# A two-layer decoder trunk on one core: heads stepped before other tasks, x turned on other engines at two places, fewer low parts on POOL

## The chip, the cores and the metric

The kernel runs on one core of one Trainium2 chip. The metric is the device time of one execution in microseconds, median over runs. TensorE is called PE in the rows, VectorE DVE, ScalarE ACT, GpSimd POOL, SyncE SP.

## The reference, cut to what matters

The input x has 256 rows (tokens) of 2048 columns; mem has 256 rows as well. Each of two layers does, all in float32:

```python
h = rmsnorm(x, g);  p = h @ W_in                # columns split among four mixers
x = x + concat(A(p), B(p), C(p), D(p)) @ W_o    # A: forgetting attention (FoX), B: latent attention (MLA),
                                                # C: spatial gating unit, D: differential attention; 4 heads each
c = rmsnorm(x, g2)
x = x + cross_attention(c, rmsnorm(mem)) @ W_co # 4 heads, 256 memory rows
f = rmsnorm(x, g3)
x = x + (silu(f @ W_gate) * (f @ W_up)) @ W_down  # hidden width 5632
```

The output is the norm of the last x. The forgetting attention adds to its scores the difference of two running sums of log-forget values, one per row and one per column.

## The kernel before, in words

**Products.** Every float32 product is made of three matmuls on numbers split into a high part (rounded to the fp32r type) and a low part (what is left): high by high, high by low of the weight, low of the activation by high (lines 303, 304 and 305 in `multiply_natural`). So each weight block of 1 MB, once fetched ("raw"), is cast by ACT into `whi` (line 204), and `wlo = raw - whi` is made by DVE, or by POOL (line 210). POOL makes it for every fourth unit of the groups whose name stands in the tuple `POOLED` near the top of the file.

**Work lists.** The kernel is a long list of groups, each one a matrix product into 512 columns of output (`dq`, `m`, `dk`, ..., `v`, `u`, `wo`, `cq`, `ck`, `cv`, `wco`, `gate`, `up`, `down`). `drive` cuts the groups into units, each of two blocks of 128 rows of the weight by 512 columns: 12 matmuls. It walks through the units in order: it first converts the weights of up to three units ahead (casts and low parts), then issues the matmuls of the unit, then calls `step()`. A group may give back some of its units to be done later ("hold"): thus the first `wco` units of two chunks are interleaved.

**Tasks.** All else (attention heads, norms, turning x) is written as Python generators that are advanced by one piece for each unit. Tasks are of two kinds: `urgent`, all of which advance in each `step()`, and `background` (heads), of which the first two advance. What `step()` issues stands in the program order of its engine right there; each engine runs its instructions strictly in that order.

**x and its norms.** x lies in four chunks of 512 columns, `self.x[0..3]`. When a `wo` or `wco` group of a chunk is done, `into_x` adds its two halves from PSUM into x on DVE (line 950, two instructions of 128x512) and starts `norm_chunk` as a task: ACT forms the sums of squares, and the chunk is then turned (columns onto partitions), since it will be a stationary operand. If the argument `early` is true, DVE turns it by `turn_blocks` in 16 instructions (line 428), four of them in each step, into an SBUF buffer `xT`. Otherwise TensorE turns it in `turn` (line 419), two groups of four 128x128 matmuls into PSUM. Both are followed by `split_turned`: high parts on ACT (line 206) and low parts on DVE (line 212), one for each 128 columns, called `cT_hi`, `cT_lo` for the cross attention and `fT_hi`, `fT_lo` for the feed-forward half. A unit that needs a chunk whose task isn't finished drains that task first (`Split.need`).

**Heads.** `scores` (lines 436 to 441) issues the score matmuls of a head, over pairs of operands; it forms the part for the second 128 queries over 256 keys, and that for the first 128 queries over 128 keys, except that operands of type fp32r are always taken with 256 columns. In the differential heads a reciprocal `inv` (line 468) of the softmax's sums is taken on DVE, ACT scales by it (line 473), TensorE turns the result (line 479). In the cross attention `cpt` (line 1078) are the turned probabilities, `cpT` (line 1079) their copy on ACT, and `co` (line 1116) the products with the values.

Of the kernel before, what the change touches and what calls it, by code (L numbers as in the profile page):

```python
# [12 lines left out]
F32R = mybir.dt.float32r  # L13
# [6 lines left out]
P = 128  # L20
T = 2
S = T * P
# [3 lines left out]
NC = 4  # L26
# [10 lines left out]
LEAD = 8  # L37
O_ORDER = [4, 5, 6, 7, 12, 13, 14, 15, 0, 1, 2, 3, 8, 9, 10, 11]
RAWS = 4
POOLED = ("wco", "wo", "cq", "fk", "fv")  # L40

PI_LO = float(np.nextafter(np.float32(np.pi), np.float32(0)))
MAGIC = 1.5 * 2.0 ** 23
# [18 lines left out]
class Task:  # L62
# [5 lines left out]
    def step(self):  # L68
        if not self.done:
            try:  # L70
                next(self.gen)
            except StopIteration:
                self.done = True
# [68 lines left out]
class Kernel:  # L142
# [48 lines left out]
            yield  # L191

    def step(self):
        for t in list(self.urgent):
            t.step()
        self.urgent = [t for t in self.urgent if not t.done]
        for t in list(self.background)[:2]:
            t.step()
        self.background = deque(t for t in self.background if not t.done)


    def high(self, src, hi, scale=None):
# [24 lines left out]
    def drive(self, groups):  # L227

        units, held = [], []
        for g in groups:  # L230
            i, own = 0, []
            for src, kper in g.blocks:
                b = Block(src, kper * g.ncols)
                step = 1 if not units and not own else 1024 // g.ncols if g.ncols in (256, 512) else 2
                for k0 in range(0, kper, step):
                    n = min(step, kper - k0)
                    own.append(Unit(g, b, k0, n, i))
                    i += n
            if g.hold:
                units, held = units + own[: g.hold], own[g.hold :]  # L240
            else:
                units, held = units + own[: len(held)] + held + own[len(held) :], []
# [23 lines left out]
    def convert(self, u):  # L266
# [15 lines left out]
        u.lo = self.whl.tile([P, 1024], F32R, tag="wlo", name="wlo")  # L282
        self.split(b.raw[:, u.k0 * u.group.ncols : u.k0 * u.group.ncols + nw], u.hi[:, :nw], u.lo[:, :nw], eng=nc.gpsimd if u.group.name in POOLED and u.i % 4 == 0 else None)

# [57 lines left out]
    def norm_chunk(self, st, c, g, name, early):  # L342

        nc, xs, stats, xc = self.nc, st[0], st[1], self.x[c]
        part = xs.parts[c] = self.split_tile(name)
        for t in range(T):
            self.square_sum(xc[:, t, :], stats[:, t, c : c + 1])
        st[4] += 1
        yield
        yield  # L350
        if early:
            raw = self.slot("xT")
            yield from self.turn_blocks(xc[:], raw)
        for b in range(2):
            tv = raw[:, 2 * b : 2 * b + 2, :] if early else self.turn(xc, 2 * b, 2, "xT")
            self.split_turned(tv, part, 2 * b, self.gains[:, g, 4 * c + 2 * b : 4 * c + 2 * b + 2])
            yield
# [75 lines left out]
    def scores(self, pairs, name="s"):  # L433

        ps = self.bank(name)
        first = True
        for q, off, nk in ((1, 0, S), (0, S, P)):
            for n, (x, y) in enumerate(pairs):
                w = S if x.dtype == F32R else nk
                self.nc.tensor.matmul(ps[:, off : off + w], x[:, q * P : (q + 1) * P], y[:, :w], start=first, stop=(q == 0 and n == len(pairs) - 1))  # L440
                first = False
        return ps

# [353 lines left out]
    def mixers(self, l, norm, st, mem):  # L797

        y = Split(4)
# [140 lines left out]
        yield group("v", False, done_v)  # L940
        yield group("u", False, done_u)
        for c in range(NC):
            yield Group("wo", self.blocks("w_o", l, c), 512, y, False, self.into_x(c, st, 1 + 3 * l, "cT", c < NC - 1), O_ORDER, begin=mem if c == NC - 1 else None, hold=0 if c else 4)

    def into_x(self, c, st=None, g=None, name=None, early=False):

# [134 lines left out]
    def cross(self, l, norm, st, memT, mres):  # L1081
        s = {}
        y, cT = Split(1), norm[0]

        def out_q(ps):
            nat = self.slot("cq", shape=(P, T, 512))
            self.out_natural(ps, 0, 512, nat, self.times(norm[2][0], 128.0 ** -0.5))
            s["q"] = self.slot("cqT")
            yield
            yield from self.turn_blocks(nat[:], s["q"])  # L1090

        def done_q(ps):
            norm[3].drain()
            s["tq"] = self.soon(out_q(ps))

        def done_k(ps):
            self.mem_rms.drain()
            kT = self.slot("ckT")
            s["tk"] = self.soon(self.out_turned(ps, kT, mres[1]))
            s["p"] = [self.slot("cpT", shape=(P, 2, 512)) for _ in range(2)]  # L1100
            s["heads"] = [self.later(self.attend_memory((s["tq"], s["tk"]), s["q"], kT, h, s["p"][h // 2][:, h % 2, :])) for h in range(4)]

        def out_v(ps, hh):
            if hh == 0:
                s["v"] = self.slot("cv", shape=(P, T, 512))
                y.parts[0] = self.split_tile("yc")
            v = s["v"]
            self.out_natural(ps, 0, 256, v[:, :, 256 * hh : 256 * hh + 256], mres[0])
            yield
            for t in s["heads"][2 * hh : 2 * hh + 2]:  # L1110
                t.drain()
            o = self.bank("co")
            for i in range(2):
                h = 2 * hh + i
                for kt in range(2):
                    self.nc.tensor.matmul(o[:, i * S : (i + 1) * S], v[:, kt, h * P : (h + 1) * P], s["p"][hh][:, i, kt * S : (kt + 1) * S], start=(i == 0 and kt == 0), stop=(i == 1 and kt == 1))
            ov = o[:].rearrange("p (i s) -> p i s", i=2)
            self.split(ov, y.parts[0][0][:, 2 * hh : 2 * hh + 2, :], y.parts[0][1][:, 2 * hh : 2 * hh + 2, :])

        def done_v(hh):  # L1120
            def f(ps):
                s["tv%d" % hh] = self.soon(out_v(ps, hh))
                if hh == 1:
                    y.tasks[0] = [s["tv0"]]
                    y.late = s["tv1"]
            return f

        yield Group("cq", self.blocks("w_cq", l), 512, cT, False, done_q)
        yield Group("ck", self.blocks("w_ck", l), 512, memT, True, done_k)
        for hh in range(2):  # L1130
            yield Group("cv", self.blocks("w_cv", l, hh, 8), 256, memT, False, done_v(hh))
        for c in range(NC):
            yield Group("wco", self.blocks("w_co", l, c), 512, y, False, self.into_x(c, st, 2 + 3 * l, "fT"), hold=0 if c else 1)


    def ffn(self, l, norm, st):
# [211 lines left out]
```

## Time and profile before

| | |
|---|---|
| median of 3 runs | 2347.46 us (2346.2 to 2347.61) |
| the profiled execution | 2347.7 us |
| its span, first to last instruction | 2346.0 us |
| mean granted clock of TensorE | 0.999 |
| busy: TensorE / DVE / ACT / POOL | 99% / 64% / 48% / 11% |

The profile's times are of one profiled execution; 1.7 us of its 2347.7 lie outside the span. Times of single instructions in the rows are microseconds from the start of the span. Matmuls overlap: one of 512 columns is listed with 0.39 us, while the next starts 0.227 us after it, so that ends of matmuls are modelled and starts are what counts.

### The profile page before, as it was taken

How to read it: one execution, taken by the hardware profiler on the slowest of the kernel's cores; microseconds unless marked ns; L12 is line 12 of the kernel's file. 1: busy time of each engine (PE TensorE's matmuls, PEld its weight loads, DVE VectorE, ACT ScalarE, POOL GpSimd, SP SyncE). 2: the span in 40 equal slices, each digit the busy share in tenths (PEclk: the TensorE clock that was granted, in tenths of full speed). 3: DMA queues.
4: the chain of work that ended last, by engine and by line, in shares of the span. 5: the costliest groups of instructions: out<-in, count | busy, mean ns of one | idle time of the engine just before them, and what ended most of it. 6: DMA issues, size and time to landing. Idle time of an engine off the chain costs nothing.

```text
span 2346.0 us, 28353 instructions
## 1 busy us (share of the span) xinstructions
PE 2324.7 (99%) x10992; PEld 1950.3 (83%) x10992; DVE 1508.6 (64%) x2175; ACT 1132.2 (48%) x1611; POOL 251.3 (11%) x182
## 2 busy tenths in 40 slices
PE   9999999999999999999999999999999999999998
PEld 8888878888888888888898888798888888888886
DVE  6856687655766446767766666866666664476564
ACT  7656555644443334444455555545444443434443
POOL 1222341100000000000012314411000000000000
PEclk9999999999999999999999999999999999999999
DMA  8654555455455555555545454554555555555643
GB/s 293 223 177 154 186 189 188 164 193 200 179 208 195 189 197 181 196 200 184 203 164 193 161 176 159 201 197 162 197 180 197 202 194 196 197 180 192 221 179 126
DMA packets 69719, 444.24 MB, mean 189 GB/s; under 512 B 8000, under 2 KB 10064, under 8 KB 19920
## 3 DMA queue, kind: packets, MB, share of 16 engines
q1 hardware_dynamic: 67328, 435.52, 52.4%
q0 software_dynamic: 2112, 6.85, 0.9%
q8 instruction: 86, 1.41, 0.2%
q14 instruction: 49, 0.40, 0.0%
q10 hardware_dynamic: 144, 0.06, 0.0%
HBM read 440.30 MB, written 2.10 MB: 189 GB/s over the span
## 4 chain that ended last, share of the span: by engine, by line
PE 88%; DVE 4%; ACT 2%; DMA 2%; issue 1%; POOL 1%; SPq 0%; POOLq 0%; ACTq 0%; DVEq 0%
PE gate L305 7%; PE gate L304 7%; PE gate L303 7%; PE up L305 7%; PE up L304 7%; PE up L303 7%; PE down L303 7%; PE down L305 7%; PE down L304 7%; DVE wlo L210 1%; PE wo L305 1%; PE wo L303 1%; PE wo L304 1%; ACT whi L204 1%; DVE xT L428 1%
## 5 line engine op out<-in xcount | busy, mean ns | idle before, releaser
L210 DVE TENSOR_TENSOR wlo<-raw,whi 128x1024 fp32r<-128x1024 f32 (+3 forms) x764 | 933.5, 1235 | 572.4 <-ACT whi L204 566.2
L204 ACT CAST whi<-raw 128x1024 fp32r<-128x1024 f32 (+2 forms) x828 | 842.3, 1037 | 633.8 <-PE up L305 246.6
L303 PE MATMUL gate<-whi,fT_hi 128*128 128x512 f32 x704 | 274.7, 390 | 0.0
L305 PE MATMUL gate<-whi,fT_lo 128*128 128x512 f32 x704 | 274.0, 389 | 0.0
L304 PE MATMUL gate<-wlo,fT_hi 128*128 128x512 f32 x704 | 273.9, 389 | 0.0
L303 PE MATMUL up<-whi,fT_hi 128*128 128x512 f32 x704 | 273.9, 389 | 0.0
L304 PE MATMUL up<-wlo,fT_hi 128*128 128x512 f32 x704 | 273.9, 389 | 0.0
L305 PE MATMUL up<-whi,fT_lo 128*128 128x512 f32 x704 | 273.9, 389 | 0.0
L303 PE MATMUL down<-whi,hid_hi 128*128 128x512 f32 x704 | 273.9, 389 | 0.0
L304 PE MATMUL down<-wlo,hid_hi 128*128 128x512 f32 x704 | 273.9, 389 | 0.0
L305 PE MATMUL down<-whi,hid_lo 128*128 128x512 f32 x704 | 273.9, 389 | 0.0
L210 POOL TENSOR_TENSOR wlo<-raw,whi 128x1024 fp32r<-128x1024 f32 x64 | 165.3, 2587 | 408.4 <-ACT whi L204 408.2
L428 DVE STREAM_TRANSPOSE hidT<-silu 32x256 f32<-32x256 f32 x352 | 153.3, 436 | 5.7
L305 PEld LDWEIGHTS down<-whi,hid_lo 128*128 128x128 f32 x704 | 132.2, 188 | 27.6
L305 PEld LDWEIGHTS gate<-whi,fT_lo 128*128 128x128 f32 x704 | 132.2, 188 | 27.5
L304 PEld LDWEIGHTS up<-wlo,fT_hi 128*128 128x128 f32 x704 | 132.2, 188 | 27.5
L303 PEld LDWEIGHTS up<-whi,fT_hi 128*128 128x128 f32 x704 | 132.2, 188 | 27.5
L305 PEld LDWEIGHTS up<-whi,fT_lo 128*128 128x128 f32 x704 | 132.2, 188 | 27.3
L304 PEld LDWEIGHTS down<-wlo,hid_hi 128*128 128x128 f32 x704 | 132.2, 188 | 27.3
L303 PEld LDWEIGHTS down<-whi,hid_hi 128*128 128x128 f32 x704 | 132.2, 188 | 27.3
L304 PEld LDWEIGHTS gate<-wlo,fT_hi 128*128 128x128 f32 x704 | 132.2, 188 | 27.2
L303 PEld LDWEIGHTS gate<-whi,fT_hi 128*128 128x128 f32 x704 | 132.2, 188 | 27.2
(426 smaller groups left out, 3347.1 us busy)
## 6 DMA issues: line engine op xcount, KB each, us to landing
raw<-in_w_gate SPq DMA_DIRECT2D x88, 1024.0 KB, 4.8
raw<-in_w_up SPq DMA_DIRECT2D x88, 1024.0 KB, 4.7
raw<-in_w_down SPq DMA_DIRECT2D x88, 1024.0 KB, 4.8
raw<-in_w_o SPq DMA_DIRECT2D x32, 1024.0 KB, 4.8
raw<-in_w_dk SPq DMA_DIRECT2D x8, 1024.0 KB, 5.1
raw<-in_w_dv SPq DMA_DIRECT2D x8, 1024.0 KB, 6.5
raw<-in_w_fq SPq DMA_DIRECT2D x8, 1024.0 KB, 4.9
raw<-in_w_fk SPq DMA_DIRECT2D x8, 1024.0 KB, 4.8
```

The lines of the kernel that those rows point to most:

```text
L204: self.nc.scalar.copy(hi, src)
L210: (eng or self.nc.vector).tensor_tensor(out=lo, in0=src, in1=hi.bitcast(F32), op=ALU.subtract)
L303: mm(o, xh, wh, start=(i == 0), stop=False)
L304: mm(o, xh, wl, start=False, stop=False)
L305: mm(o, xl, wh, start=False, stop=(i == len(g.ks) - 1))
L428: self.nc.vector.transpose(o[:, :, :, a, :], src[32 * a : 32 * a + 32, :, :, b, :])
```

## The change

It has six parts:

1. `wo` and `cq` leave `POOLED`: all their low parts are made by DVE.
2. `step()` advances the two background tasks (heads) first and the urgent tasks after them.
3. In `norm_chunk`, a chunk turned on DVE waits one more step between the last transpositions and the split.
4. In `scores`, the second part has 128 columns for operands of type fp32r too.
5. After `wo`, all four chunks are turned on TensorE (before, chunks 0 to 2 on DVE).
6. After `wco`, chunks 0 and 1 are turned on DVE (before, all four on TensorE).

```diff
--- before.py
+++ after.py
@@ -37,7 +37,7 @@
 LEAD = 8
 O_ORDER = [4, 5, 6, 7, 12, 13, 14, 15, 0, 1, 2, 3, 8, 9, 10, 11]
 RAWS = 4
-POOLED = ("wco", "wo", "cq", "fk", "fv")
+POOLED = ("wco", "fk", "fv")
 
 PI_LO = float(np.nextafter(np.float32(np.pi), np.float32(0)))
 MAGIC = 1.5 * 2.0 ** 23
@@ -191,12 +191,12 @@
             yield
 
     def step(self):
+        for t in list(self.background)[:2]:
+            t.step()
+        self.background = deque(t for t in self.background if not t.done)
         for t in list(self.urgent):
             t.step()
         self.urgent = [t for t in self.urgent if not t.done]
-        for t in list(self.background)[:2]:
-            t.step()
-        self.background = deque(t for t in self.background if not t.done)
 
 
     def high(self, src, hi, scale=None):
@@ -351,6 +351,7 @@
         if early:
             raw = self.slot("xT")
             yield from self.turn_blocks(xc[:], raw)
+            yield
         for b in range(2):
             tv = raw[:, 2 * b : 2 * b + 2, :] if early else self.turn(xc, 2 * b, 2, "xT")
             self.split_turned(tv, part, 2 * b, self.gains[:, g, 4 * c + 2 * b : 4 * c + 2 * b + 2])
@@ -436,8 +437,7 @@
         first = True
         for q, off, nk in ((1, 0, S), (0, S, P)):
             for n, (x, y) in enumerate(pairs):
-                w = S if x.dtype == F32R else nk
-                self.nc.tensor.matmul(ps[:, off : off + w], x[:, q * P : (q + 1) * P], y[:, :w], start=first, stop=(q == 0 and n == len(pairs) - 1))
+                self.nc.tensor.matmul(ps[:, off : off + nk], x[:, q * P : (q + 1) * P], y[:, :nk], start=first, stop=(q == 0 and n == len(pairs) - 1))
                 first = False
         return ps
 
@@ -940,7 +940,7 @@
         yield group("v", False, done_v)
         yield group("u", False, done_u)
         for c in range(NC):
-            yield Group("wo", self.blocks("w_o", l, c), 512, y, False, self.into_x(c, st, 1 + 3 * l, "cT", c < NC - 1), O_ORDER, begin=mem if c == NC - 1 else None, hold=0 if c else 4)
+            yield Group("wo", self.blocks("w_o", l, c), 512, y, False, self.into_x(c, st, 1 + 3 * l, "cT"), O_ORDER, begin=mem if c == NC - 1 else None, hold=0 if c else 4)
 
     def into_x(self, c, st=None, g=None, name=None, early=False):
 
@@ -1130,7 +1130,7 @@
         for hh in range(2):
             yield Group("cv", self.blocks("w_cv", l, hh, 8), 256, memT, False, done_v(hh))
         for c in range(NC):
-            yield Group("wco", self.blocks("w_co", l, c), 512, y, False, self.into_x(c, st, 2 + 3 * l, "fT"), hold=0 if c else 1)
+            yield Group("wco", self.blocks("w_co", l, c), 512, y, False, self.into_x(c, st, 2 + 3 * l, "fT", c < 2), hold=0 if c else 1)
 
 
     def ffn(self, l, norm, st):
```

In the changed file the lines from 354 to 438 stand one higher than before (line 428 is now 429, 419 is 420), the later ones where they were. At three places the order of an engine's instructions shows what moved. In the names, the number behind `x` is the chunk (`x0_113` is chunk 0 of x).

**DVE, end of `wco`, first layer.** `fT_lo_4099`, `fT_lo_4125` and `fT_lo_4195` are the low parts of chunks 0, 1 and 2, the `wlo` are those of the first `gate` weights. Before:

```order
L212 SCALAR_TENSOR_TENSOR fT_lo_4099<-xT_4147,gains_91,fT_hi_4098 128x256 x2
L210 TENSOR_TENSOR wlo_4159<-raw_3957,whi_4158 128x1024
L950 TENSOR_TENSOR x2_115<-wco_4134,x2_115 128x512 x2
L212 SCALAR_TENSOR_TENSOR fT_lo_4099<-xT_4176,gains_91,fT_hi_4098 128x256 x2
L212 SCALAR_TENSOR_TENSOR fT_lo_4125<-xT_4185,gains_91,fT_hi_4124 128x256 x2
L210 TENSOR_TENSOR wlo_4201<-raw_3957,whi_4200 128x1024
L212 SCALAR_TENSOR_TENSOR fT_lo_4125<-xT_4217,gains_91,fT_hi_4124 128x256 x2
L210 TENSOR_TENSOR wlo_4229<-raw_4061,whi_4228 128x1024
L950 TENSOR_TENSOR x3_116<-wco_4204,x3_116 128x512 x2
L212 SCALAR_TENSOR_TENSOR fT_lo_4195<-xT_4246,gains_91,fT_hi_4194 128x256 x2
```

After; `fT_lo_4161` are low parts of chunk 2, `fT_lo_4078` those of chunk 0, which the first `gate` unit multiplies:

```order
L429 STREAM_TRANSPOSE xT_4126<-x0_113 32x2x4x32 x4
L429 STREAM_TRANSPOSE xT_4155<-x1_114 32x2x4x32 x4
L210 TENSOR_TENSOR wlo_4167<-raw_3918,whi_4166 128x1024
L429 STREAM_TRANSPOSE xT_4126<-x0_113 32x2x4x32 x4
L429 STREAM_TRANSPOSE xT_4155<-x1_114 32x2x4x32 x4
L210 TENSOR_TENSOR wlo_4194<-raw_4040,whi_4193 128x1024
L950 TENSOR_TENSOR x3_116<-wco_4170,x3_116 128x512 x2
L429 STREAM_TRANSPOSE xT_4126<-x0_113 32x2x4x32 x4
L429 STREAM_TRANSPOSE xT_4155<-x1_114 32x2x4x32 x4
L212 SCALAR_TENSOR_TENSOR fT_lo_4161<-xT_4219,gains_91,fT_hi_4160 128x256 x2
L210 TENSOR_TENSOR wlo_4235<-raw_4040,whi_4234 128x1024
L212 SCALAR_TENSOR_TENSOR fT_lo_4078<-xT_4126,gains_91,fT_hi_4077 128x256 x4
```

The transpositions of chunks 0 and 1 (line 429) have come onto DVE, four in a step; chunk 0's last four and its low parts stand behind the add of chunk 3, where before chunk 0's low parts stood around the add of chunk 2.

**TensorE, the second pair of heads of the cross attention, first layer**, the piece of the difference where `cpt` moves (a `-` row is of the kernel before, a `+` row of the changed one):

```order
-L305 MATMUL cv<-whi,memTs_lo 128x256
-L1078 MATMUL cpt<-ident,cp 128x128 x8
 L303 MATMUL wco<-whi,yc_hi 128x512
 L304 MATMUL wco<-wlo,yc_hi 128x512
@@ -2055,4 +2060,5 @@
 L304 MATMUL wco<-wlo,yc_hi 128x512
 L305 MATMUL wco<-whi,yc_lo 128x512
+L1078 MATMUL cpt<-ident,cp 128x128 x8
 L1116 MATMUL co<-cpT,cv 128x256 x4
 L303 MATMUL wco<-whi,yc_hi 128x512
```

`cpt` has moved down by one unit of `wco`, to right in front of the `co` that reads its copy; the same holds for the first pair, and for both in the second layer.

**DVE, the stage of `u`, first layer**: `inv` is the reciprocal for a differential head, `v` the gating unit's norm, `yd_lo` low parts of finished heads. Before:

```order
L777 SCALAR_TENSOR_TENSOR v<-v,lnr,lnw 128x512
L212 SCALAR_TENSOR_TENSOR yd_lo<-ydT,gsm,yd_hi 128x512
L468 RECIPROCAL inv<-sums 128x2
L212 SCALAR_TENSOR_TENSOR yd_lo<-ydT,gsm,yd_hi 128x512
L210 TENSOR_TENSOR wlo<-raw,whi 128x1024
```

After:

```order
L210 TENSOR_TENSOR wlo<-raw,whi 128x1024
L429 STREAM_TRANSPOSE ydT<-on 32x2x4x32 x4
L468 RECIPROCAL inv<-sums 128x2
L776 SCALAR_TENSOR_TENSOR v<-v,mv,lnw 128x512
L777 SCALAR_TENSOR_TENSOR v<-v,lnr,lnw 128x512
L210 TENSOR_TENSOR wlo<-raw,whi 128x1024
L212 SCALAR_TENSOR_TENSOR yd_lo<-ydT,gsm,yd_hi 128x512
```

The reciprocal has moved ahead of two instructions for `v` and of the first `yd_lo`.

## Rows read from the trace of the kernel before

**Rows 1.** The page, part 1: busy time, share of the span, instructions.

```profile
PE 2324.7 (99%) x10992; PEld 1950.3 (83%) x10992; DVE 1508.6 (64%) x2175; ACT 1132.2 (48%) x1611; POOL 251.3 (11%) x182
```

**Rows 2.** The page, chain that ended last, by engine.

```profile
PE 88%; DVE 4%; ACT 2%; DMA 2%; issue 1%; POOL 1%; SPq 0%; POOLq 0%; ACTq 0%; DVEq 0%
```

**Rows 3.** Waits of PE: us in total, times, longest us.

```profile
PE wo L304 <- DVE wlo L210: 3.5, 4, 1.5
PE fpt L479 <- ACT fp L473: 3.0, 2, 1.5
PE cq L304 <- POOL wlo L210: 1.2, 3, 0.6
PE fo L500 <- ACT fptt L483: 1.1, 2, 0.6
```

**Rows 4.** Timeline of PE in wo: start us, us, engine, instruction [idle before].

```profile
323.45 0.39 PE L303 MATMUL wo<-whi,ys_hi 128*128 128x512 f32 x1
...
325.30 0.50 PE L304 MATMUL wo<-wlo,ys_hi 128*128 128x512 f32 x1 [1.46 <-DVE wlo L210]
325.63 0.40 PE L305 MATMUL wo<-whi,ys_lo 128*128 128x512 f32 x1
```

**Rows 5.** Timeline of DVE and POOL in wo.

```profile
314.61 2.96 POOL L210 TENSOR_TENSOR wlo<-raw,whi 128x1024 fp32r<-128x1024 f32 x1 [3.28 <-ACT whi L204]
...
315.23 5.16 DVE L212 SCALAR_TENSOR_TENSOR cT_lo<-xT,gains,cT_hi 128x256 fp32r<-128x256 f32 x2
...
325.27 1.79 DVE L428 STREAM_TRANSPOSE xT<-x 32x256 f32<-32x256 f32 x4
```

**Rows 6.** Timeline of DVE and PE in the stage of u.

```profile
248.11 0.75 DVE L777 SCALAR_TENSOR_TENSOR v<-v,lnr,lnw 128x512 f32<-128x512 f32 x1
...
249.44 0.16 DVE L468 RECIPROCAL inv<-sums 128x2 f32<-128x2 f32 x1
...
250.55 0.33 PE L479 MATMUL fpt<-ident,fp 128*128 128x128 f32 x1 [1.51 <-ACT fp L473]
```

**Rows 7.** Lines by form, DVE and ACT: busy us, mean ns, idle before.

```profile
L210 DVE TENSOR_TENSOR wlo<-raw,whi 128x1024 fp32r<-128x1024 f32 x724 | 899.0, 1254 | 553.2 <-ACT whi L204 547.4
...
L428 DVE STREAM_TRANSPOSE xT<-x 32x256 f32<-32x256 f32 x144 | 62.7, 436 | 2.2
...
L212 DVE SCALAR_TENSOR_TENSOR fT_lo<-xT,gains,fT_hi 128x256 fp32r<-128x256 f32 x32 | 13.8, 478 | 3.1 <-ACT fT_hi L206 3.1
...
L204 ACT CAST whi<-raw 128x1024 fp32r<-128x1024 f32 x788 | 813.3, 1051 | 621.1 <-PE up L305 246.6 <-PE down L305 203.4 <-PE gate L305 116.5
...
L206 ACT ACTIVATE fT_hi<-xT,gains 128x256 fp32r<-128x256 f32 x32 | 13.2, 472 | 11.1 <-PE xT L419 11.1
```

**Rows 8.** Timeline of PE and ACT, first heads of the cross attention.

```profile
411.24 1.04 PE L1078 MATMUL cpt<-ident,cp 128*128 128x128 f32 x8
...
412.17 1.07 ACT L1079 COPY cpT<-cpt 128x512 f32<-128x512 f32 x2
```

**Rows 9.** Lines by form, PE: scores of FoX.

```profile
L440 PE MATMUL fs<-rows,own 128*128 128x256 f32 x16 | 6.1, 384 | 0.0
```

**Rows 10.** Timeline of DVE in wco.

```profile
444.01 1.22 DVE L210 TENSOR_TENSOR wlo<-raw,whi 128x1024 fp32r<-128x1024 f32 x1 [1.95 <-ACT whi L204]
...
454.12 1.28 DVE L950 TENSOR_TENSOR x<-wco,x 128x512 f32<-128x512 f32 x2
```

**Rows 11.** Timeline of PE from wco to gate.

```profile
453.37 0.60 PE L419 MATMUL xT<-ident,x 128*128 128x128 f32 x4
453.73 0.48 PE L303 MATMUL gate<-whi,fT_hi 128*128 128x512 f32 x1
```

**Rows 12.** Cores: span and mean granted clock of PE.

```profile
core 0: 2346.0 us, clock 0.999
```

**Rows 13.** Timeline of PE at the start.

```profile
1.11 3.79 PE L588 MATMUL idle<-ones 128*128 128x128 f32 x16 [1.11 <-DVE mhalf L584]
...
6.49 0.39 PE L303 MATMUL dq<-whi,hT_hi 128*128 128x512 f32 x1
```

## The prediction, made before the change was run

> **What bounds the kernel now.** First the page's busy times: TensorE is busy for 2324.7 of 2346.0 us [rows 1]. The reader is to see that hardly 1% is left to gain by better cover, and that any time in which TensorE stands is lost whole. Then the chain of waits: 88% of it is TensorE [rows 2]. Third, TensorE's waits by releaser, which name every place where it stands. Four kinds matter here, 11 waits: 3.5 us in wo for a low part on DVE, 3.0 in u for a softmax, 1.2 in cq for a low part on POOL, 1.1 in front of fo [rows 3]. The rest is a steady stream: a matmul of 512 columns starts every 0.227 us (each weight matrix is worked off in units of 12 such matmuls, 12 x 0.227 = 2.72 us).
>
> **What such a wait really costs** is read from two starts. In wo a matmul starts at 323.45 and the one two places on at 325.63: 2.18 us where 2 x 0.227 = 0.45 is normal, so 1.72 lost where the list says 1.46 [rows 4]. The ends are modelled, so I add 0.26 to each listed wait.
>
> **The change, part by part.**
>
> *POOL without wo and cq.* 32 low parts of wo and 8 of cq go to DVE at 1.25 us each [rows 7]. What they leave behind is the reason for the waits: while POOL writes a low part for 2.96 us, two instructions of DVE beside it take 5.16 us [rows 5], where the same shape takes 2 x 0.478 undisturbed [rows 7]. With that gone I count wo's waits (3.5 + 4 x 0.26 = 4.5) and cq's (1.2 + 3 x 0.26 = 2.0) as gained. The 40 x 1.25 = 50 us on DVE are hidden as long as DVE, 64% busy [rows 1], keeps ahead of TensorE in wo and cq; it is rid there of the 2 x 3 x 16 = 96 transpositions of the fourth part below. If that cover is gone, the 6.5 us stay.
>
> *Heads first in a step.* In u the softmax's reciprocal stands on DVE behind v (0.75 us) and a low part of yd, at 249.44, and TensorE's fpt waits for it until 250.55 [rows 6]. The order after the change puts the reciprocal ahead of both, about 1.5 us earlier, which is the whole wait: 3.0 + 2 x 0.26 = 3.5 gained in two layers. In front of fo another matmul pair of 0.65 us now stands between the transposition and its reader, nearly the whole of each wait; 1.1 + 2 x 0.26 less 0.1 each = 1.4 gained. On the other side, the order puts co's first four matmuls directly behind the eight transpositions of cpt, in four places. Before, a unit lay between: cpt at 411.24, its copies on ACT from 412.17 [rows 8], a unit of matmuls, and then co. A copy is half of 1.07 = 0.54 us, ends about 0.3 us after the transpositions in the best case and later by one copy at worst; I take 0.5 for each: **+2.0** (bounds 0.5 and 4).
>
> *Scores with 128 columns.* 8 of the 16 matmuls of 128x256 [rows 9] become 128x128. None can give back more than half of its 384 ns, 8 x 0.19 = 1.5 in all; but matmuls overlap, and matmuls of 128x128 start 0.13 us apart [rows 8], about a third of 384 ns as it is, so most of that isn't there to be had. If the weight load behind a short one shows, it costs at most that 0.13, 1.0 in all. Between -1.5 and +1.0 I take 0.
>
> *Chunks for the cross attention on TensorE, two of the four for the feed-forward half on DVE.* 3 x 2 groups of four transpositions come to TensorE in each layer and 2 x 2 leave it: 4 more groups over both layers. A group takes 453.37 to 453.73, 0.36, and a slower start of the next matmul, 0.1 [rows 11]: 4 x 0.45 = **+1.8**.
>
> *The new wait, at gate.* Here the change costs most. The first gate unit needs chunk 0's high and low parts. Until now TensorE turned it. Now DVE does, in 16 instructions, four in a step, and the order shows the last four on DVE behind the add of chunk 3, the last of the stage. I lay DVE's queue out from where it last waits, the low part that starts at 444.01 [rows 10]; each four transpositions take 1.79 [rows 5] and a low part 1.25 [rows 7], an add of two halves 1.28 [rows 10]:
> - low part until 445.3, 4 of chunk 0 until 447.1, low part 448.3, add of chunk 2 449.6, 4 + 4 transpositions 453.2, low part 454.4, 4 + 4 458.0, low part 459.2, add of chunk 3 460.5;
> - 4 + 4 464.1 (chunk 0 is complete at 462.3), two low parts of chunk 2 at 0.48 465.0, low part 466.2, first low part of chunk 0 466.7.
>
> TensorE's side: before, the wco stage ended with four transpositions at 453.37, and gate began at 453.73 [rows 11]. Four groups of transpositions (chunks 0 and 1) fall away from that stretch, 4 x 0.45 = 1.8, so gate could begin at 451.9. Its first two matmuls need high parts alone; the third, due 2 x 0.227 later at 452.4, needs the low part. 466.7 - 452.4 = **14.3 us** lost.
>
> The third gate unit needs chunk 1. After the wait TensorE has 10 matmuls, a group of transpositions, a unit and the first group of chunk 3: 466.7 + 2.27 + 0.45 + 2.72 + 0.45 = 472.6, and the matmul with the low part is due at 473.1. But ACT has chunk 1's high parts behind those of chunk 3, which wait for that group, and a cast; DVE has a weight's low part ahead. From 472.6: two high parts 0.94 [rows 7], the cast 1.05 [rows 7], the weight's low part 1.25, chunk 1's 0.48, and some 0.5 for the steps between the engines: 476.8, so **3.7 us**. Together 18.0 a layer, **+36.0**.
>
> At least so much is lost: chunk 3 can't be added before TensorE has finished it, 454.12 [rows 10] less 1.8 = 452.3; then the add 1.28, eight transpositions 3.58, two low parts of chunk 2 0.96, a low part 1.25 and chunk 0's 0.48 end at 459.9, even with an empty queue ahead: 7.5 us.
>
> The price of a transposition decides the queue: 28 lie between 445.3 and 466.7. The rows have 436 ns for one [rows 7], and four in 1.79 us [rows 5]. The Trainium skill ("VectorE: DVE Perf Modes", section "The three transpose paths") gives VectorE 311 ns and TensorE 390 for a transposition; by an estimate from its 311, 28 of them would take 8.7 us and not 12.5, the wait 10.5 and the total 7.6 less than mine, 2373.9. The trace's row is for this very instruction, so I go by it.
>
> *The clock.* TensorE has no long stop in the run before; its mean granted clock was 0.999 [rows 12]. What it does after standing is seen only at the start: 16 transposition-size matmuls in 3.79 us, 0.24 each from 1.11 on [rows 13], where eight later take 1.04, 0.13 each [rows 8]: half speed, the lower of its two levels; at 6.49 a matmul takes 0.39 us [rows 13], as everywhere later. So some 5.4 us ran at half speed: 2.7 lost. I take a stop of 14 us to be like that start, once a layer: **+5.4** (bounds 0, and 10.8 if the wait for chunk 1 does the same). The Trainium skill ("TensorE: Matmul & The Clock Gate", section "Why this matters for your kernels") warns of idle gaps between bursts of matmuls, since the clock falls in them; no row of this trace has such a gap in mid-run, and without that the sum is the first rival's.
>
> **The sum**, against the profiled execution's 2347.7 us (0.24 above the median of 2347.46; the difference is left out): gains 4.5 + 2.0 + 3.5 + 1.4 = 11.4; 2347.7 - 11.4 + 2.0 + 1.8 + 36.0 + 5.4 = **2381.5 us**, 1.4% slower.
>
> **The rivals.**
> - *The clock holds through the gap*: 2381.5 - 5.4 = 2376.1. For it: only the cold start shows the lower level. Against: a stop of 14 us is longer than anything in the run. 0.22.
> - *The gains don't come*: DVE, with 50 us more, is late in wo and cq as often as now, and the softmax waits too. 2381.5 + 11.4 = 2392.9. For it: the waits in wo are on DVE's low parts already [rows 3]. Against: the DVE instructions there are stretched by POOL, not queued [rows 5]. 0.12.
> - *DVE's queue is empty in front of chunk 3*: the wait is the least one, 7.5 + 3.7 a layer, 22.4 in both and not 36.0: 2367.9. For it: casts on ACT may come sooner. Against: the adds alone and 28 transpositions fill it. 0.08.
> - *The other side: chunk 0 is turned in time.* DVE would have to finish chunk 0's transpositions before 449.7 (452.4 less two low parts of chunk 2, 0.96, a weight's 1.25 and its own 0.48). Then gate doesn't wait, the clock stays, and 2347.7 - 11.4 + 3.8 = 2340.1, faster by 0.3%. It decides at whether the last four stand ahead of chunk 3's add; the order says behind it, and the least wait above rests on that. 0.03.
>
> **How the numbers follow.** The forecast has 0.53, its own range is 2376 to 2387 (the bounds of co and the wait's 2 us a layer); 0.02 is left for what I don't see. The range, 2367 to 2394, takes in the forecast and the first three rivals. The measurement of this kernel can tell some 0.2%, 4.7 us, from no change: faster by more than that 0.03, within it 0.02, slower 0.95.
>
> **What would show it.** In the waits of TensorE: gate L305 (or L304) waiting for DVE's fT_lo twice a layer, some 14 and 3.7 us; the busy share of TensorE down by 1.5%; the granted clock below 0.999 after each stop; co waiting for the copy four times by half a microsecond; no waits in wo, fpt and cq. The DVE timeline should show transpositions without gaps from 445 to 464. I'm wrong if gate's first wait is under 7 us, or if TensorE still stands in wo and u.

## The result, and the profile after

The changed kernel takes 2382.16 us (median of 4 runs, 2381.27 to 2382.58), the kernel before in the same sessions 2347.09. The ratio is 1.0149, with a 95% interval of 1.0132 to 1.0167: slower by 1.5%. The forecast was 2381.5.

The page's first part of the changed kernel, beside [rows 1]:

```profile
span 2380.6 us, 28299 instructions
...
PE 2333.5 (98%) x11008; PEld 1956.6 (82%) x11008; DVE 1504.9 (63%) x2183; ACT 1132.3 (48%) x1611; POOL 145.0 (6%) x142
```

DVE is busy no longer than before (1504.9 us against 1508.6) although it took over 40 low parts from POOL (251 us of POOL became 145): it lost 32 transpositions on balance, and its instructions in wo are no longer stretched (a `cT_lo` of the first layer takes 480 ns on average, 746 before). So the work moved without a bill on DVE. Of the 34.6 us that the span grew, 25.8 are time in which TensorE stands; the other 8.8 are busy time of TensorE, which has 16 more transpositions (4 groups) and, as is seen below, matmuls at a lower clock. That is why its busy share fell by 1.1 points only and not by the 1.5 of the forecast. The waits of TensorE in the changed kernel (us in total, times, longest):

```profile
PE gate L303 <- ACT fT_hi L206: 25.9, 4, 10.7
PE gate L305 <- DVE fT_lo L212: 5.4, 3, 2.5
PE fo L500 <- ACT fptt L483: 2.0, 4, 0.6
...
PE co L1116 <- ACT cpT L1079: 1.0, 4, 0.2
```

Against [rows 3] the lines of wo, fpt and cq are gone, fo's has doubled, co is new, and gate stands at the top with 31 us. Its timeline on TensorE in the first layer (start us, us, instruction, idle before), beside [rows 11]:

```profile
449.89 0.60 PE L420 MATMUL xT<-ident,x 128*128 128x128 f32 x4
461.16 0.79 PE L303 MATMUL gate<-whi,fT_hi 128*128 128x512 f32 x1 [10.67 <-ACT fT_hi L206]
...
464.86 0.80 PE L305 MATMUL gate<-whi,fT_lo 128*128 128x512 f32 x1 [2.48 <-DVE fT_lo L212]
465.45 0.63 PE L303 MATMUL gate<-whi,fT_hi 128*128 128x512 f32 x1
465.88 0.63 PE L304 MATMUL gate<-wlo,fT_hi 128*128 128x512 f32 x1
...
469.12 0.60 PE L420 MATMUL xT<-ident,x 128*128 128x128 f32 x4
...
472.32 0.60 PE L420 MATMUL xT<-ident,x 128*128 128x128 f32 x4
475.18 0.50 PE L303 MATMUL gate<-whi,fT_hi 128*128 128x512 f32 x1 [2.27 <-ACT fT_hi L206]
...
476.43 0.80 PE L305 MATMUL gate<-whi,fT_lo 128*128 128x512 f32 x1 [0.48 <-DVE fT_lo L212]
...
480.09 0.60 PE L420 MATMUL xT<-ident,x 128*128 128x128 f32 x4
```

The transpositions at 449.89 would have let gate begin 0.36 later, as before, and the matmul that needs the low part at 450.70; it begins at 464.86. That is 14.2 us. At the third unit the same count goes from 472.32 to a due 473.13, and the matmul begins at 476.43: 3.3 us. The second layer has the same two stops, 14.2 and 3.3 us. Behind the first stop starts lie 0.43 us apart (465.45 to 465.88), not 0.227: the granted clock is 0.50 of full from 465.4 to 468.9, 1.00 from 469.2 to 472.3, and again 0.50 from 476.4 to 479.1. DVE's timeline shows what kept the data:

```profile
443.59 1.77 DVE L429 STREAM_TRANSPOSE xT<-x 32x256 f32<-32x256 f32 x4
445.39 1.23 DVE L210 TENSOR_TENSOR wlo<-raw,whi 128x1024 fp32r<-128x1024 f32 x1
446.53 1.28 DVE L950 TENSOR_TENSOR x<-wco,x 128x512 f32<-128x512 f32 x2
447.85 3.57 DVE L429 STREAM_TRANSPOSE xT<-x 32x256 f32<-32x256 f32 x8
451.45 1.22 DVE L210 TENSOR_TENSOR wlo<-raw,whi 128x1024 fp32r<-128x1024 f32 x1
452.70 3.58 DVE L429 STREAM_TRANSPOSE xT<-x 32x256 f32<-32x256 f32 x8
456.32 1.23 DVE L210 TENSOR_TENSOR wlo<-raw,whi 128x1024 fp32r<-128x1024 f32 x1
457.46 1.28 DVE L950 TENSOR_TENSOR x<-wco,x 128x512 f32<-128x512 f32 x2
458.77 3.62 DVE L429 STREAM_TRANSPOSE xT<-x 32x256 f32<-32x256 f32 x8
...
464.32 1.66 DVE L212 SCALAR_TENSOR_TENSOR fT_lo<-xT,gains,fT_hi 128x256 fp32r<-128x256 f32 x4
```

No idle time stands in any row: DVE works from 443.59 on without a pause. Its last transpositions of chunk 0 stand behind the add of chunk 3 at 457.46, and chunk 0's low parts start at 464.32, behind four transpositions of chunk 1, two low parts of chunk 2 and a weight's low part. And the stretch on ACT from which fo's waits come, first in the kernel before, then in the changed one (`fptt` is the copy of a head's turned probabilities, which fo reads):

```profile
274.86 0.48 ACT L483 COPY fptt<-fpt 128x384 f32<-128x384 f32 x1 [0.99 <-PE fpt L481]
276.54 0.80 ACT L473 ACTIVATE fp<-fp,inv 128x256 f32<-128x256 f32 x2 [1.19 <-DVE inv L468]
```

```profile
276.61 0.80 ACT L473 ACTIVATE fp<-fp,inv 128x256 f32<-128x256 f32 x2 [1.43 <-DVE inv L468]
...
277.83 1.04 ACT L204 CAST whi<-raw 128x1024 fp32r<-128x1024 f32 x1
278.77 0.47 ACT L483 COPY fptt<-fpt 128x384 f32<-128x384 f32 x1
279.14 1.04 ACT L204 CAST whi<-raw 128x1024 fp32r<-128x1024 f32 x1
280.09 0.47 ACT L483 COPY fptt<-fpt 128x384 f32<-128x384 f32 x1
```

Both copies that fo reads now stand behind the cast of a weight, 1.04 us each, and the first one also behind the scaling of the second head (276.61), ahead of which it stood before.

From the starts of all matmuls in both traces (each gap less the usual gap behind such a matmul, summed by the group that came late) the account reads, in us over both layers:

| place | forecast | measured |
|---|---|---|
| gate, stops and clock | 36.0 + 5.4 = +41.4 | +40.6 |
| wo | -4.5 | -4.6 |
| cq | -2.0 | -3.1 |
| fpt | -3.5 | -2.8 |
| fo | -1.4 | +1.6 |
| co | +2.0 | +2.0 |
| scores | 0 | 0 |
| groups of transpositions | +1.8 | +1.8 (4 more, by their price) |

The measured column sums to +35.5, the span grew by 34.6; the rest is scattered over the start of the kernel and small waits. That the forecast of 2381.5 lies within 1 us of the result is in part luck: gate was put 0.8 us too high and cq's gain 1.1 too low, while fo and fpt were put 3.0 and 0.7 too low, and these errors partly cancel. The scores' zero is read directly: from the first of a head's six FoX matmuls to the second matmul behind them it takes 1.122 us before and 1.117 after, in six of the eight heads (in the other two other small matmuls stood right ahead before, and it went from 1.207 to 1.118).

### The profile page after: what moved, and what is told of

The parts are those of the page before. It is cut to its first block, busy times and chain, and to the rows that moved or that the text cites. A ratio compares the mean times of both kernels' runs of the same rounds, so it can differ in the third digit from the quotient of the medians.

```text
span 2380.6 us, 28299 instructions
## 1 busy us (share of the span) xinstructions
PE 2333.5 (98%) x11008; PEld 1956.6 (82%) x11008; DVE 1504.9 (63%) x2183; ACT 1132.3 (48%) x1611; POOL 145.0 (6%) x142
## 4 chain that ended last, share of the span: by engine, by line
PE 91%; DVE 5%; ACT 2%; POOL 1%; issue 1%; DMA 0%; SPq 0%; POOLq 0%; DVEq 0%; ACTq 0%
PE gate L305 7%; PE gate L303 7%; PE gate L304 7%; PE up L304 7%; PE up L303 7%; PE up L305 7%; PE down L303 7%; PE down L305 7%; PE down L304 7%; PE wo L305 2%; PE wo L303 2%; PE wo L304 2%; DVE wlo L210 1%; PE m L303 1%; PE m L305 1%
## 5 line engine op out<-in xcount | busy, mean ns | idle before, releaser
L210 DVE TENSOR_TENSOR wlo<-raw,whi 128x1024 fp32r<-128x1024 f32 (+2 forms) x804 | 966.3, 1216 | 563.7 <-ACT whi L204 556.3
L336 ACT ACTIVATE junk<-x 128x512 f32<-128x512 f32 x56 | 35.4, 632 | 109.0 <-DVE x L950 82.4
```

Of the source, the lines that this page charges most:

```text
L210: (eng or self.nc.vector).tensor_tensor(out=lo, in0=src, in1=hi.bitcast(F32), op=ALU.subtract)
L336: self.nc.scalar.activation(junk[:, : src.shape[-1]], src, AF.Square, accum_out=acc)
```

## The experiments

Theory: gate stops since chunk 0 is turned on DVE, at the end of a full queue, and the lowered clock adds to it. Rival: DVE is late because it also has wo's and cq's low parts and takes the heads first; the turned chunk only shows it.

**Part 6 undone, and part 6 alone.** To the changed kernel (lines are cut here and below to what changes):

```diff
-self.into_x(c, st, 2 + 3 * l, "fT", c < 2), hold=0 if c else 1)
+self.into_x(c, st, 2 + 3 * l, "fT"), hold=0 if c else 1)
```

> The changed kernel with all chunks for the feed-forward half turned on TensorE again (part 6 undone). Theory (gate stops because chunk 0 is turned on DVE): the stops in gate vanish, 40.6 us by the starts in the trace, and 8 groups of transpositions come back to TensorE, 8 x 0.45 = 3.6: 2382.2 - 40.6 + 3.6 = 2345. Rival (DVE is late because it has wo's and cq's low parts and the heads come first; turning chunk 0 only shows it): half of the stop or more stays, over 2360.

Measured 2345.84 us, beside 2347.42 of the kernel before (ratio 0.9993, 0.9984 to 1.0003). TensorE waits nowhere in gate. The theory's 2345 is met, the rival falls: the other five parts together make no difference that can be measured.

The same line put into the kernel before, alone:

> The kernel before with part 6 alone (chunks 0 and 1 for the feed-forward half turned on DVE). Theory: the same stops as in the changed kernel, 2347.1 + 40.6 - 3.6 = 2384, give or take 4 since the extra step of part 3 is absent. Rival (the other parts make DVE late): under 2360.

Measured 2376.21 (1.0124, 1.0107 to 1.0140): the stop is there without any other part, so the rival falls again, but the time is 8 us under the theory's, outside its margin of 4. The waits of this kernel say why:

```profile
PE gate L303 <- ACT fT_hi L206: 21.3, 2, 10.7
PE gate L305 <- DVE fT_lo L212: 5.0, 2, 2.5
```

Two times each, not four and three: the first stop is the same to 0.01 us, the one at the third unit is absent. This kernel lacks part 3, and the next run asks whether that is the reason.

**The extra step of part 3.** To the changed kernel:

```diff
             yield from self.turn_blocks(xc[:], raw)
-            yield
```

> The changed kernel without the extra step of part 3. Theory (that step puts chunk 1's high parts on ACT behind those of chunk 3 and a cast, and so makes the second stop, 3.1 us, and the lowered clock after it, some 1.4): no stop at the third gate unit, the first stop as long as ever: 2382.2 - 2 x 4.5 = 2373. Rival (the second stop is chunk 1's late transpositions): 2382.

Measured 2375.21 (1.0119, 1.0106 to 1.0133); the waits in gate are 21.3 and 4.9 us, two of each. So the second stop is a matter of part 3: with the extra step the high parts of chunk 1 are issued on ACT behind a cast and the first ones of chunk 3, without it half of them are ahead of both. ACT's timeline of the changed kernel (the first ones of chunk 3 at 472.95, those of chunk 1 at 474.62), then of this run (half of chunk 1's at 471.83, the first ones of chunk 3 at 473.69):

```profile
472.95 0.84 ACT L206 ACTIVATE fT_hi<-xT,gains 128x256 fp32r<-128x256 f32 x2 [1.42 <-PE xT L420]
473.68 1.04 ACT L204 CAST whi<-raw 128x1024 fp32r<-128x1024 f32 x1
474.62 1.71 ACT L206 ACTIVATE fT_hi<-xT,gains 128x256 fp32r<-128x256 f32 x4
```

```profile
471.83 0.91 ACT L206 ACTIVATE fT_hi<-xT,gains 128x256 fp32r<-128x256 f32 x2
473.69 0.84 ACT L206 ACTIVATE fT_hi<-xT,gains 128x256 fp32r<-128x256 f32 x2 [0.95 <-PE xT L419]
```

By the starts gate lost 7.6 us less; the rest of the expected 9 came back as 1 us of waits in front of transpositions.

**One chunk in place of two.** To the changed kernel:

```diff
-"fT", c < 2)
+"fT", c < 1)
```

> The changed kernel with only chunk 0 turned on DVE for the feed-forward half. Theory (the length of the stop is DVE's queue from 443 us on, of which chunk 1's 12 transpositions are 5.4 us, less two low parts that come instead): the first stop is 10 us and not 14, the one for chunk 1 goes; 2382.2 - 2 x (4 + 3.1 + 1.5 of clock - 0.9 of transpositions) = 2367. Rival (the stop depends on the place behind chunk 3's add alone): the first stop stays at 14, 2375.

Measured 2367.02 (1.0083, 1.0068 to 1.0098). The theory's number. TensorE's timeline:

```profile
450.93 0.60 PE L420 MATMUL xT<-ident,x 128*128 128x128 f32 x4
459.18 0.80 PE L303 MATMUL gate<-whi,fT_hi 128*128 128x512 f32 x1 [7.65 <-ACT fT_hi L206]
...
461.07 0.80 PE L305 MATMUL gate<-whi,fT_lo 128*128 128x512 f32 x1 [0.67 <-DVE fT_lo L212]
```

The low part was due at 450.93 + 0.81 = 451.74 and came 9.3 us late, where two chunks made it 14.2. Chunk 0 stands at the same place behind chunk 3's add in both; what shortened the stop is the shorter queue: the add itself starts at 455.48 and not at 457.46, and behind it four transpositions stand and not eight.

**The clock.** To the changed kernel, ahead of the first gate group of each layer (lines cut):

```diff
+        def busy():
+            idle = self.tbank("idle")
+            for i in range(92):
+                nc.tensor.matmul(idle[:, :P], self.ones[:], self.ones[:], start=(i == 0), stop=(i == 91))
...
-done_gate)
+done_gate, begin=busy if j == 0 else None)
```

> The changed kernel with 92 products of ones by ones (128x128, about 10 us) issued on TensorE between the last transpositions of wco and the first gate matmul of each layer: extra work, nothing left out. Theory (the chip grants the lower clock after the stop, and that costs 2.2 us a layer behind the first one): the first gate matmuls run 0.227 us apart and not 0.43, 2382.2 - 4.4 = 2377.8, less yet if the stop at the third unit no longer starts from a lowered clock. If stops of 2.5 us alone lower the clock: 2382. Rival (the matmuls behind the stop are slow since their operands come late): 2382, and the starts stay 0.43 apart at full granted clock.

Measured 2391.88 (1.0190, 1.0174 to 1.0205): a miss of the experiment. The 92 products are 184 matmuls in the trace and took 20.7 us, so they ended 9.6 us after the data. Half as many:

> As fill_gap, with 46 products in place of 92, since each takes two matmuls in the trace: 46 x 2 x 0.1125 = 10.4 us, which just fills the stop of 10.8. Theory (clock): gate's first matmuls start 0.227 apart, the time falls by 2.2 us a layer at least, 2377.8 or less. Rival (stops of 2.5 us alone bring the lower clock): 2382.

Measured 2382.68 (1.0149, 1.0134 to 1.0165), the rival's number. The timeline shows two halves of an answer:

```profile
452.11 10.44 PE L1143 MATMUL idle<-ones 128*128 128x128 f32 x92
462.94 0.50 PE L303 MATMUL gate<-whi,fT_hi 128*128 128x512 f32 x1 [0.40 <-ACT fT_hi L206]
463.28 0.40 PE L304 MATMUL gate<-wlo,fT_hi 128*128 128x512 f32 x1
466.64 0.80 PE L305 MATMUL gate<-whi,fT_lo 128*128 128x512 f32 x1 [2.96 <-DVE fT_lo L212]
```

Behind the filled stretch the first two matmuls run at the upper level, 0.34 apart with the start. Then TensorE stands for 2.96 us, and behind that it is at the lower one, as in the windows of this run (the second last of the numbers without unit is the granted clock, PEclk; rows are stretches):

```profile
core 0: us, PE busy (x) PEld busy (x) DVE busy (x) ACT busy (x) POOL busy (x), PEclk, DMA share, GB/s
452.10:462.50 10.40, 10.40 (x94) 10.25 (x92) 10.08 (x20) 3.53 (x9) 0.00 (x0) 1.00 0.27 102
463.80:466.60 2.80, 0.00 (x0) 0.00 (x0) 2.79 (x6) 0.29 (x1) 0.00 (x0) 1.00 0.00 0
466.70:469.70 3.00, 3.00 (x7) 2.42 (x8) 2.82 (x7) 0.00 (x0) 0.00 (x0) 0.50 0.77 276
```

The granted clock is 0.50 of full in the last stretch, 1.2 GHz and not 2.4. So all four stretches had to be filled:

> The changed kernel with products of ones by ones in all four stretches in which TensorE stands in front of a layer's first three gate units: 46 ahead of the first matmul, 13 ahead of the third, 11 ahead of the third unit, 2 ahead of its third matmul; extra work, nothing left out. It measures the clock's share by itself: the data come no sooner, only the clock has no reason to fall. Theory (5.6 us of the 40.6 in gate are the lowered clock): granted clock 0.999, gate's matmuls 0.227 apart, 2382.2 - 5.6 = 2376.6. Rival (the clock costs nothing by itself, since the data set the pace): 2382.

Measured 2380.70 (1.0144, 1.0127 to 1.0161), between the two. The filling overshot: the 13 products had to wait themselves (in the row, for DVE's `fT_lo`) and ended late,

```profile
462.91 4.77 PE L315 MATMUL idle<-ones 128*128 128x128 f32 x26 [1.53 <-DVE fT_lo L212]
467.43 0.48 PE L310 MATMUL gate<-whi,fT_lo 128*128 128x512 f32 x1
...
469.83 0.60 PE L430 MATMUL xT<-ident,x 128*128 128x128 f32 x4
...
477.14 0.50 PE L310 MATMUL gate<-whi,fT_lo 128*128 128x512 f32 x1
...
479.55 0.60 PE L430 MATMUL xT<-ident,x 128*128 128x128 f32 x4
```

so the total doesn't give the clock's price. The stretches behind do: from the third matmul to the next transpositions it is 2.40 us here (467.43 to 469.83), against 4.26 in the changed kernel (464.86 to 469.12), and 2.41 against 3.66 at the third unit. 1.86 + 1.25 = 3.1 us in this layer is what the lower level cost. The same starts of the second layer give 3.92 less 2.39 and 3.47 less 2.42, 2.6 us: **5.7 us** in both layers. That is also what is left of gate's 40.6 us when the four stops, 34.9, are taken off.

**The other parts.** To the kernel before, part 1 alone (`POOLED = ("wco", "fk", "fv")`):

> The kernel before with part 1 alone (POOL without low parts in wo and cq). Theory (the waits in wo and cq come from POOL's low parts stretching DVE's instructions): wo and cq no longer wait, 7.7 us by the starts: 2347.4 - 7.7 = 2339.7. Rival (DVE with 50 us more and its transpositions still there is late itself): 2344 or more, with waits for DVE's wlo in wo.

Measured 2347.84 (1.0004, 0.9995 to 1.0013): the rival's. Its waits:

```profile
PE wo L304 <- DVE wlo L210: 2.2, 4, 0.9
PE cq L304 <- DVE wlo L210: 1.7, 2, 0.9
PE xT L419 <- DVE x L950: 1.6, 4, 0.5
```

POOL no longer stretches anything there (a `cT_lo` takes 477 ns, 746 before), but with the 40 low parts and the transpositions DVE itself is late. With part 5 as well (`"cT"` without `c < NC - 1`):

> Parts 1 and 5 alone (POOL without wo and cq; all chunks for the cross attention turned on TensorE). Theory: as a_pool, with 12 more groups of transpositions on TensorE, 12 x 0.45 = 5.4: 2345.1. If part 5 is what ends the waits (rival of a_pool), this is the faster of the two.

Measured 2345.04 (0.9992, 0.9983 to 1.0001), the theory's number: no waits in wo and cq, and the price is 12 groups on TensorE. Part 1 gives its 7.7 us only where DVE is rid of something, and part 5 takes 5.4 of them back.

Part 2 alone (the heads first in each step):

> The kernel before with part 2 alone (heads first in each step). Theory, from the starts in the changed kernel's trace: fpt's wait in u goes (-2.8), fo waits twice a layer and not once (+1.6), co waits four times (+2.0): 2347.0 + 0.8 = 2347.8, no change that can be measured. Rival (the prediction's step, fo's wait goes as well): 2344.8.

Measured 2348.24 (1.0005, 0.9996 to 1.0014): as expected, nothing. By the starts fpt -2.8, fo +1.6, co +2.0. But the theory had fo's part by luck. Its two waits behind ACT's casts aren't in this run; another one stands in their place, earlier, in front of an earlier head's fo (1.2 us, once a layer):

```profile
PE fo L500 <- DVE u L789: 2.4, 2, 1.2
```

Here POOL still makes low parts for wo. Beside one of 2.86 us a `yd_lo` of 128x512 on DVE took 2.89 us (0.74 in the changed kernel), `u` came behind it, and fo waited for `u`. So what the order of the heads costs fo depends on what else is late beside it; b_two below, with the heads first in u and without those low parts on POOL, has no such wait. No run takes part 2 alone out of the changed kernel.

**A version that beats both.** Part 1; two chunks for the cross attention on DVE; the heads first only in u's units; nothing else:

```diff
-"cT", c < NC - 1)
+"cT", c < 2)
...
-            self.step()
+            self.step(u.group.name)
...
+        if name == "u":
+            self.step_heads()
```

> Meant to beat both: parts 1 and half of 5 (chunks 0 and 1 for the cross attention on DVE, 2 and 3 on TensorE), the heads first only while u's units run, nothing of parts 3, 4, 6. Theory: DVE has 2 x 16 transpositions less than in a_pool behind which its low parts were late, so wo and cq don't wait (-7.7 at most), 4 groups come to TensorE (+1.8), fpt doesn't wait (-2.8), fo and co are as before: 2338.3. Rival (DVE is still late): wo and cq keep some 4 us, 2343.

Measured 2338.69 (0.9964, 0.9950 to 0.9977). With one chunk (`c < 1`):

> As b_two, with chunk 0 alone on DVE for the cross attention. Theory: no waits in wo and cq, 8 groups come to TensorE (+3.6): 2347.0 - 7.7 + 3.6 - 2.8 = 2340.1. Slower than b_two if two chunks on DVE are no longer late, faster if they are.

Measured 2340.37 (0.9971, 0.9960 to 0.9983). Both come out as summed from the single parts (expected 2338.3 and 2340.1), and both beat the kernel before. Waits in wo, cq, co and fpt are absent in both, fo's single one stays at 1.1 us. The two intervals of the ratios overlap, but the single times, taken in the same sessions, don't (2338.32 to 2339.36 with two chunks, 2339.54 to 2341.46 with one). The medians differ by 1.7 us, where the groups on TensorE give 4 x 0.45 = 1.8. So two chunks are likely better than one; with 5 and 6 runs it isn't firmly shown.

## Why the prediction was right, point by point

- **The stop at gate** was forecast at 14.3 us and measured at 14.2, the queue on DVE step by step: forecast ends of chunk 2's and 3's adds 449.6 and 460.5, measured 447.8 and 458.7; all of the changed trace is some 1.7 us sooner there, TensorE's side too. Undoing part 6 takes it away, part 6 alone brings it, and a shorter queue shortens it. The reason is the program order of one engine, and that could be read before the run.
- **The second stop** was forecast at 3.7 and measured at 3.3. The reason given, ACT's order, is right; that this order is the work of part 3's extra step the prediction didn't say, and u_step and a_ft_dve showed it.
- **The price of a transposition.** The rows' 436 ns hold: the changed trace has eight in 3.57 us, 0.446 each. By the 311 ns of the Trainium skill ("VectorE: DVE Perf Modes", section "The three transpose paths") the total would have been 2373.9, by estimate; the measurement decides for the row. That section of the Trainium skill gives the figure for 128x128 in bf16, and the instruction here has 32x256 in f32; the prediction used it as the price of this instruction without saying so.
- **The clock** was taken at 2.7 us once a layer, like the start of the kernel. It fell twice in each layer, behind both stops, at 1.86 and 1.25 us in the first and 1.53 and 1.05 in the second, 5.7 in all where 5.4 was forecast. The sum is near by luck: the length of the slow stretch was too long, the number of them too small. The rule of the Trainium skill ("TensorE: Matmul & The Clock Gate", section "Why this matters for your kernels") that gaps bring the clock down agrees with these rows.
- **POOL without wo and cq**: wo -4.6 (forecast -4.5), cq -3.1 (-2.0; two short waits, of some 0.2 us each, that the list didn't show but the starts do). The cover was said to be the removed transpositions; a_pool shows that without them most of the gain isn't there.
- **Heads first**: fpt (-2.8, forecast -3.5) and co (+2.0) about as forecast. **The step that failed is fo**: "another matmul pair of 0.65 us now stands between the transposition and its reader, nearly the whole of each wait". The pair is itself a reader that waits: its copy on ACT, made at 274.86 before, is made at 278.77, behind the second head's scaling and a cast of 1.04 us, and the other copy behind one more cast, at 280.09. So two waits a layer (0.60 and 0.40 us in the first) stand in place of one, +1.6 and not -1.4 (in the changed kernel; in a_heads the same +1.6 is another wait). I had read the order on TensorE alone, not on ACT, which makes the copy.
- Of the rivals, "the gains don't come" was wrong only because parts 1 and 5 came together, and the other side, chunk 0 turned in time, couldn't come: the add of chunk 3 stands ahead.

## What to carry to other kernels

To move work from a full engine to one that is 63% busy on average can still stop the full one, if the work's result is due at the end of a stage, where the other engine's queue is longest: lay out that queue from the program order, with durations from rows, before believing the busy share. A part that frees an engine and a part that needs it free are worth something only together, so try them in pairs, and drop the halves that take the gain back. Where a task is moved ahead, read the order on every engine that its chain passes, copies and casts included. And where a time comes out as expected, see in the list of waits that it is the expected wait: in a_heads it was another one.

## What the runs showed that was not expected

- A score matmul of 128 columns in place of 256 as the last of a head gives nothing: 1.117 us against 1.122 for the whole group, though its columns are half as many.
- A stop of 2.96 us, after 10 us of full work, was followed by 3 us at a granted clock of 0.50 (fill_46); in the changed kernel the stop of 2.27 us with two matmuls and 0.48 us behind it was too.
- One step more or less for a task that isn't late itself (part 3) costs 7 us in the changed kernel, through the order on ACT at one place in each layer.
